# First convolution taps on ScalarE, more taps by adding transfers, and sevens in other groups of a hybrid attention and convolution block

## The chip, the cores and the metric

The kernel runs on one core of one Trainium2 chip. A core has TensorE (PE in the profile; PEld is its weight load), VectorE (DVE), ScalarE (ACT), GpSimd (POOL) and SyncE (SP). SP, ACT and POOL also issue transfers (DMA). The metric is the device time of one execution in microseconds; lower is better.

## The reference

One layer for 256 positions and width 4096, all in float32:

```python
xn = rms_norm(h, norm_in_g[i])
proj = xn @ w_in[i]                      # 4096 x 14336
q, k, v, z_a, a_c, g_c, z_c = split(proj)   # each 2048 wide
y_a = chunked_attention(q, k, v, rel_table[i])        # 16 heads of 128
y_a = rms_norm(y_a, attn_out_g[i]) * silu(z_a)
u = a_c * sigmoid(g_c)
u = causal_depthwise_conv(u, w_dw) + b_dw             # 31 taps
u = silu(layer_norm(u, ln_g, ln_b))
y_c = rms_norm(u @ w_pw + b_pw, conv_out_g[i]) * silu(z_c)
h = h + concatenate([y_a, y_c]) @ w_out[i]
gate = sigmoid(rms_norm(h, ple_norm_g[i]) @ w_ple_gate[i] + b_ple_gate[i])
h = h + gate * (p[i] @ w_ple[i])
return rms_norm(h, final_g)
```

## The kernel before

**Products.** A float32 operand is split into a high and a low part (`wh`, `wl` for weights, `big_t` for activations); a product of two blocks is three matmuls of 128x512 (high by high, low by high, high by low; line 428). ScalarE makes the high part by a cast, VectorE the low part by a subtraction (lines 204, 205). Weight parts have three buffers each.

**Groups.** `mixed_product` computes two column blocks of 512 over 16 pairs of k-blocks. A pair is done as an *eight* (8 block products, 24 matmuls) or, by Winograd's form of Strassen's method, as a *seven* (7 block products, 21 matmuls). A seven needs sums of weight blocks (`ua`, `ub`; VectorE, lines 526 to 540) and, for the activations, a combination (`xS`, `comb`), which has to be made beforehand. The string tables (`early`, `early_seven` and so on) give the order of the pairs in a group: a number with `*` is a seven whose sums VectorE makes, one with `+` a seven whose first sum comes from a plain transfer and an adding transfer on GpSimd's queue (line 471), a bare number an eight.

**Stages of the first half.** Ten groups follow one another: convolution chunk 0 (`glu_conv(0)`), chunk 1, query and key heads 0, value heads 0 and 1, chunk 2, query and key 1, chunk 3, query and key 2, query 3 with value 2, and key and value 3 (order `norm`). After the fourth, sixth, ninth and tenth group `attention(g)` runs for four heads: scores on TensorE, maxima on VectorE, exponential on ScalarE, transposes and values on TensorE, with copies on ScalarE between. After the tenth group and `attention(3)` comes the pointwise product (`w_pw`), whose left operand is `uS`, the split of the swish of the layer norm.

**The fill queue.** The convolution is 31 taps for each of 16 blocks of channels, on VectorE (`conv_tap`, lines 791 and 795). `glu_conv` puts a chunk's 124 taps into the queue `later`. After each pair of a group `fill(n)` takes the next `n` pieces from it; `n` comes from a table (`early_fills`, `six_fills`, `seven_fills`, `norm_fills`), one number for each pair. `layer_norm_swish` puts 71 pieces behind the taps: sums, the mean (a matmul), centering and squares, the variance (a matmul, and a power on GpSimd), its spread (a matmul), 16 swishes and 16 splits into `uS`, with empty places between. What is left after `attention(3)` is done by one `fill(len(later))`.

**Order.** A scheduler below the kernel interleaves the instructions of neighbouring pieces; each engine then runs its own in that fixed order and waits where it must. `behind_cast` places a piece behind the latest weight cast.

Of the kernel before, what the change touches and what calls it, by code (L numbers as in the profile page):

```python
# [10 lines left out]
F32 = mybir.dt.float32  # L11
F32R = mybir.dt.float32r
# [4 lines left out]
P = 128  # L17
# [8 lines left out]
def hybrid_block(  # L26
# [332 lines left out]
    early = units("1 3 5 0+ 7 9 2+ 11 13 4+ 15 8 6+ 10 12 14")  # L359
    early_five = units("1 3 5 0+ 7 9 2+ 11 4* 13 6+ 15 8* 10 12 14")  # L360
# [16 lines left out]

    def combine_into_places(pair, tiles):

        rows = sum_rows()  # L380
        places[pair] = spare_places(tiles[:4])
        t, i = tiles[pair // 2], pair % 2 * 2
        combine_again(None, None, t, i, rows, at_places=places[pair])()
# [266 lines left out]

    def first_pairs(add):
# [86 lines left out]
        later.extend(combinations(0))  # L738
        return n_x + 1, behind
# [49 lines left out]
    def conv_tap(cv, uT, i, b, k):  # L789
        if k == PAD:  # L790
            nc.vector.tensor_scalar(
                cv[:, i, :], uT[:, i, :], dw[:, b, k : k + 1], bdw[:, b : b + 1], ALU.mult, ALU.add
            )
        else:
            nc.vector.scalar_tensor_tensor(  # L795
                cv[:, i, PAD - k :], uT[:, i, : T + k - PAD], dw[:, b, k : k + 1],
                cv[:, i, PAD - k :], ALU.mult, ALU.add,
            )

    def comb_place(where, tag, **kw):  # L800
        return where.tile([P, 2, 2, T], F32R, tag=tag, name="comb_x", **kw), 0

    def more_combinations(pair):

        if pair in (7, 9, 11):
            c = (pair + 1) // 2
            xS[2 * c] = comb_place(act, "act") if c < 6 else comb_place(spool, "hd", bufs=5)
            later.extendleft(reversed(combinations(c)))

    def glu_conv(c):  # L810
# [4 lines left out]
        else:  # L815
            sg, gate = scaled_pair(
                w_in0, o_a + c * NB, o_g - o_a,
                *((early, r_x, early_fills) if c == 1 else (early_seven, r_x, seven_fills)),
                ahead=more_combinations if c == 2 else None,
# [616 lines left out]
```

## Time and profile before

| | |
|---|---|
| median of 3 runs | 2023.68 us (2023.65 to 2024.45) |
| the profiled execution's own time | 2023.59 us |
| its span in the trace | 2021.8 us |
| bytes by DMA | 450.86 MB, mean 223 GB/s |
| ACT_TABLE_LOAD instructions | 10, 1283 ns each |

A row of the groups reads: line, engine, operation, result <- operands, shapes, count | busy us, mean ns of one | idle time of the engine just before them and what ended it. A row of the windows reads: stretch, its length, busy us of PE, PEld, DVE, ACT, POOL with instruction counts, granted TensorE clock, DMA share, GB/s. A row of the timeline has start and length in us, engine, line and operation; neighbouring instructions of one kind are merged (xN), and an instruction's length holds a tail that overlaps the next one's start. A row of the waits reads: who waited <- for whom: us in total, times, longest.

### The profile page before, as it was taken

How to read it: one execution, taken by the hardware profiler on the slowest of the kernel's cores; microseconds unless marked ns; L12 is line 12 of the kernel's file. 1: busy time of each engine (PE TensorE's matmuls, PEld its weight loads, DVE VectorE, ACT ScalarE, POOL GpSimd, SP SyncE). 2: the span in 40 equal slices, each digit the busy share in tenths (PEclk: the TensorE clock that was granted, in tenths of full speed). 3: DMA queues.
4: the chain of work that ended last, by engine and by line, in shares of the span. 5: the costliest groups of instructions: out<-in, count | busy, mean ns of one | idle time of the engine just before them, and what ended most of it. 6: DMA issues, size and time to landing. Idle time of an engine off the chain costs nothing.

```text
span 2021.8 us, 26364 instructions
## 1 busy us (share of the span) xinstructions
PE 2003.7 (99%) x9043; PEld 1650.4 (82%) x9043; DVE 1920.5 (95%) x2759; ACT 1259.6 (62%) x1634; POOL 75.8 (4%) x83
## 2 busy tenths in 40 slices
PE   9999999999999999999999999999999999999997
PEld 7888888878888888788888888888888888888885
DVE  7999999899999999888999999999999999999997
ACT  7655555665666556776566676776666766566564
POOL 0000000000000000000000000000000000000000
PEclk9999999999999999999999999999999999999998
DMA  8788878678668877556686786876767766767675
GB/s 292 224 233 241 249 221 251 179 220 259 200 198 256 255 201 241 161 178 206 204 238 213 221 244 203 255 232 203 242 209 238 231 197 208 237 214 237 219 238 172
DMA packets 175920, 450.86 MB, mean 223 GB/s; under 512 B 14494, under 2 KB 17710, under 8 KB 175786
## 3 DMA queue, kind: packets, MB, share of 16 engines
q1 hardware_dynamic: 161952, 417.93, 63.6%
q0 software_dynamic: 13184, 30.41, 8.8%
q8 instruction: 71, 1.16, 0.2%
q10 hardware_dynamic: 650, 0.84, 0.1%
q14 instruction: 63, 0.52, 0.1%
HBM read 441.78 MB, written 4.19 MB: 221 GB/s over the span
## 4 chain that ended last, share of the span: by engine, by line
PE 93%; DVE 3%; DMA 2%; issue 2%; ACT 1%; POOLq 0%; POOL 0%; ACTq 0%; DVEq 0%
PE acc L428 70%; PE acc_P L428 18%; PE tmp_ps L170 1%; DVE wl L205 1%; PE acc L245 1%; DMA wt<-in_w_in_dram 1%; DVE cv L795 1%; DMA low<-in_w_in_dram 0%; DVE ul L205 0%; PE tmp_ps L967 0%; PE tmp_ps L951 0%; PE tmp_ps L985 0%; PE tmp_ps L990 0%; DMA wt<-in_w_ple_dram 0%; DMA wt<-in_w_ple_gate_dram 0%
## 5 line engine op out<-in xcount | busy, mean ns | idle before, releaser
L428 PE MATMUL acc<-wh,big_t 128*128 128x512 f32 x4028 | 1240.7, 391 | 0.9 <-DVE z L1146 0.9
L204 ACT CAST wh<-wt 128x1024 fp32r<-128x1024 f32 (+1 forms) x716 | 684.2, 965 | 460.9 <-PE acc L428 336.0
L428 PEld LDWEIGHTS acc<-wh,big_t 128*128 128x128 f32 x4028 | 753.5, 188 | 156.5 <-issue 1.0
L205 DVE TENSOR_TENSOR wl<-wt,wh 128x1024 fp32r<-128x1024 f32 (+1 forms) x716 | 787.9, 1112 | 30.0 <-ACT wh L204 24.8
L428 PE MATMUL acc<-wl,big_t 128*128 128x512 f32 x1958 | 760.3, 392 | 0.2 <-DVE wl L205 0.2
L428 PEld LDWEIGHTS acc<-wl,big_t 128*128 128x128 f32 x1958 | 367.4, 188 | 77.3 <-DVE wl L205 1.5
L204 ACT CAST uh<-ua 128x1024 fp32r<-128x1024 f32 x187 | 196.7, 1052 | 125.3 <-DVE ua L527 71.2
L205 DVE TENSOR_TENSOR ul<-ua,uh 128x1024 fp32r<-128x1024 f32 x187 | 228.0, 1219 | 6.7 <-ACT uh L204 5.1
L795 DVE SCALAR_TENSOR_TENSOR cv<-uT,dw,cv 128x255 f32<-128x255 f32 (+23 forms) x480 | 203.2, 461 | 1.1
L428 PE MATMUL acc_P<-uh,big_t 128*128 128x512 f32 x570 | 175.4, 389 | 0.0
L204 ACT CAST uh<-ub 128x1024 fp32r<-128x1024 f32 x99 | 104.2, 1053 | 51.6 <-DVE ub L540 36.8
L428 PEld LDWEIGHTS acc_P<-uh,big_t 128*128 128x128 f32 x570 | 107.0, 188 | 22.2
L205 DVE TENSOR_TENSOR ul<-ub,uh 128x1024 fp32r<-128x1024 f32 x99 | 120.7, 1219 | 0.5
L428 PE MATMUL acc_P<-ul,big_t 128*128 128x512 f32 x285 | 111.1, 390 | 0.0
L526 DVE TENSOR_TENSOR ua<-wt 128x512 f32<-128x512 f32 x112 | 76.7, 685 | 12.6 <-DMA wt<-in_w_in_dram 6.3
L428 PE MATMUL acc<-uh,big_t 128*128 128x512 f32 x286 | 88.5, 389 | 0.0
L428 PE MATMUL acc_P<-wh,big_t 128*128 128x512 f32 x286 | 88.2, 390 | 0.0
L527 DVE TENSOR_TENSOR ua<-wt 128x512 f32<-128x512 f32 x112 | 76.7, 685 | 4.7 <-DMA wt<-in_w_in_dram 3.5
L428 PE MATMUL acc_P<-uh,comb_t 128*128 128x512 f32 x228 | 70.2, 390 | 0.2 <-ACT uh L204 0.2
L540 DVE TENSOR_TENSOR ub<-ub,wt 128x512 f32<-128x512 f32 x99 | 68.1, 688 | 1.6
L539 DVE TENSOR_TENSOR ub<-ua,wt 128x512 f32<-128x512 f32 x99 | 67.7, 684 | 0.0
L428 PEld LDWEIGHTS acc_P<-ul,big_t 128*128 128x128 f32 x285 | 53.5, 188 | 12.1 <-DVE ul L205 1.0
(254 smaller groups left out, 1634.2 us busy)
## 6 DMA issues: line engine op xcount, KB each, us to landing
wt<-in_w_in_dram SPq DMA_DIRECT2D x416, 512.0 KB, 4.7
wt<-in_w_out_dram SPq DMA_DIRECT2D x128, 512.0 KB, 4.4
wt<-in_w_ple_gate_dram SPq DMA_DIRECT2D x128, 512.0 KB, 4.4
wt<-in_w_pw_dram SPq DMA_DIRECT2D x32, 512.0 KB, 4.5
ua<-in_w_in_dram SPq DMA_DIRECT2D x31, 512.0 KB, 4.3
ua<-in_w_in_dram POOLq DMA_DIRECT2D x31, 512.0 KB, 8.7
wt<-in_w_in_dram SPq DMA_DIRECT2D x31, 256.0 KB, 2.8
low<-in_w_in_dram POOLq DMA_DIRECT2D x12, 512.0 KB, 8.5
```

Source lines behind the costliest of these rows:

```text
L170: nc.tensor.transpose(pt[:, i * T + h * P : i * T + (h + 1) * P], src[:, h, b] if len(src.shape) == 4 else src[:, h, b * P : (b + 1) * P], ...
L204: nc.scalar.copy(wh[:, :kc, :], wt[:, :kc, :]),
L205: nc.vector.tensor_tensor(wl[:, :kc, :], wt[:, :kc, :], wh[:, :kc, :].bitcast(F32), ALU.subtract),
L245: nc.tensor.matmul(acc, a, b[:, k, :], start=kb == 0 and kind == 0, stop=kb == kblocks - 1 and kind == 2,)
L428: nc.tensor.matmul(banks[name], a, b, start=name not in begun, stop=final and ends[name] == n and kind == 2 and not (left and name in "P2 ...
L526: plus(ua[:, 0], w0[:, 0], w0[:, 1])
L527: plus(ua[:, 1], w0[:, 1], w1[:, 1])
L539: plus(ub[:, 0], ua[:, 0], w1[:, 1])
L540: plus(ub[:, 1], ub[:, 0], w1[:, 0])
L795: nc.vector.scalar_tensor_tensor(cv[:, i, PAD - k :], uT[:, i, : T + k - PAD], dw[:, b, k : k + 1], cv[:, i, PAD - k :], ALU.mult, ALU.add,)
```

## The change

- The first tap of each block (the one that also adds the bias) is done by ScalarE.
- In each chunk, blocks 2 and 3 get their taps 1 to 8 in another way: ScalarE multiplies into a tile (`tap`, two buffers shared with attention's `pT`), and a transfer on GpSimd's queue adds the tile to `cv`. One such piece stands behind every third tap of blocks 0 and 1; the remaining taps of blocks 2 and 3 come last, placed behind the latest VectorE tap.
- The combination of pair 8 is made in the first group, into spare places and a tile of its own; those of pairs 10 and 12 are made in chunks 2 and 3.
- Five groups (chunk 1, query and key 0, value 0 and 1, query and key 1, query and key 2) use `early_five` with five sevens in place of `early` with four; chunk 2 uses `early_six` in place of `early_seven`.
- The fill tables of these groups are new.

```diff
-    early_five = units("1 3 5 0+ 7 9 2+ 11 4* 13 6+ 15 8* 10 12 14")
+    early_five = units("1 3 5 0+ 7 9 2+ 11 8* 13 4+ 15 10 6* 12 14")
...
-    early_fills = (5, 6, 1, 5, 6, 1, 5, 6, 1, 5, 6, 1, 2, 5, 5, 4)
-    six_fills = (6, 6, 1, 5, 1, 5, 1, 5, 1, 5, 1, 5, 1, 6, 7, 7)
-    seven_fills = (6, 6, 1, 5, 1, 5, 1, 5, 1, 5, 1, 2, 5, 2, 5, 7)
+    five_fills = (5, 5, 1, 4, 5, 1, 4, 1, 5, 1, 4, 5, 1, 2, 5, 5)
+    third_fills = (5, 5, 4, 4, 4, 4, 5, 4, 4, 4, 4, 4, 4, 4, 5, 6)
+    early_fills = (5, 6, 1, 5, 6, 1, 5, 1, 5, 1, 4, 6, 1, 2, 6, 5)
+    six_fills = (6, 5, 1, 5, 1, 5, 1, 5, 1, 4, 1, 5, 1, 5, 6, 6)
+    seven_fills = (6, 5, 1, 5, 1, 5, 1, 5, 1, 5, 1, 2, 5, 2, 4, 7)
...
     def conv_tap(cv, uT, i, b, k):
         if k == PAD:
-            nc.vector.tensor_scalar(
-                cv[:, i, :], uT[:, i, :], dw[:, b, k : k + 1], bdw[:, b : b + 1], ALU.mult, ALU.add
+            nc.scalar.activation(
+                cv[:, i, :], uT[:, i, :], AF.Identity,
+                scale=dw[:, b, k : k + 1], bias=bdw[:, b : b + 1],
             )
...
+    def tap_by_dma(cv, uT, c, i, shift):
+
+        b = 4 * c + i
+        t = spool.tile([P, T], F32, tag="pT", name="tap")
+        nc.scalar.activation(
+            t[:, shift:], uT[:, i, : T - shift], AF.Identity,
+            scale=dw[:, b, PAD - shift : PAD - shift + 1],
+        )
+        nc.gpsimd.dma_start(cv[:, i, shift:], t[:, shift:], accum_op=ALU.add)
...
+    early_groups = {
+        1: (early_five, r_x, five_fills, None),
+        2: (early_six, r_x, third_fills, more_combinations(9, 10)),
+        3: (early_seven, r_x, seven_fills, more_combinations(11, 12)),
+    }
...
-        for i in range(4):
-            for k in reversed(range(TAPS)):
-                later.append(partial(conv_tap, cv, uT, i, 4 * c + i, k))
+        chain = {i: [partial(conv_tap, cv, uT, i, 4 * c + i, k) for k in reversed(range(TAPS))] for i in range(4)}
+        later.extend(chain[i].pop(0) for i in range(4))
+        rounds = deque((i, shift) for shift in range(1, BY_DMA + 1) for i in (2, 3))
+        for i in (2, 3):
+            del chain[i][:BY_DMA]
+        for n, work in enumerate(chain[0] + chain[1]):
+            later.append(work)
+            if n % 3 == 2 and rounds:
+                later.append(partial(behind_cast, tap_by_dma, cv, uT, c, *rounds.popleft()))
+        later.append(partial(behind_tap, chain[2].pop(0)))
+        later.extend(chain[2])
+        later.append(partial(behind_tap, chain[3].pop(0)))
+        later.extend(chain[3])
...
-    heads((o_q, 0), (o_k, 0))
-    heads((o_v, 0), (o_v, 1))
+    heads((o_q, 0), (o_k, 0), order=early_five, fills=five_fills)
+    heads((o_v, 0), (o_v, 1), order=early_five, fills=five_fills)
...
-    moved = comb_place(spool, "hd", bufs=5)
-    nc.scalar.copy(moved[0], xS[10][0])
-    xS[10] = moved
```

Counted over the program, TensorE has 12 matmuls of 128x512 less; VectorE 64 taps and 16 first taps less, 26 additions on 128x512 and 8 `ul` more; ScalarE 80 activations, 8 `uh` and 6 table loads more (16 in place of 10); GpSimd's queue 64 transfers more and 5 `ua` less.

The order of the instructions moves at the boundary between the tenth group and the pointwise product. On ScalarE, before, from the copies of the last key heads (`kT`) on, where `comb_u` is the combination of `uS` and `wh` a weight of the pointwise product:

```order
L956 COPY kT<-tmp_ps 128x512 x2
L298 CAST comb_u<-comb 128x2x256
L978 ACT_TABLE_LOAD
L978 ACTIVATE s,den<-s,nm 128x128
L978 ACTIVATE s,den<-s,nm 128x256
L204 CAST wh<-wt 128x1024
L987 COPY pT<-tmp_ps 128x384
L298 CAST comb_u<-comb 128x2x256
L204 CAST wh<-wt 128x1024
L994 ACTIVATE qT<-tmp_ps,den 128x128 x2
```

And now (line numbers of the changed kernel), where L966 is the swish, L1034 the exponential of attention, L1043 and L1050 its copies:

```order
L1012 COPY kT<-tmp_ps 128x512 x2
L966 ACT_TABLE_LOAD
L966 ACTIVATE cv<-cv,prm 128x256
L1034 ACT_TABLE_LOAD
L1034 ACTIVATE s,den<-s,nm 128x128
L1034 ACTIVATE s,den<-s,nm 128x256
L966 ACT_TABLE_LOAD
L966 ACTIVATE cv<-cv,prm 128x256
L1043 COPY pT<-tmp_ps 128x384
L966 ACTIVATE cv<-cv,prm 128x256 x3
L1050 ACTIVATE qT<-tmp_ps,den 128x128 x2
L966 ACTIVATE cv<-cv,prm 128x256 x2
```

The 16 swishes and the 16 splits stood ahead of the `kT` copies and now stand between the steps of the last four heads; the next weight cast comes behind all of them.

On TensorE at the same boundary, before (`acc_8124` to `acc_8127` belong to the pointwise product, L951 and L966 to L992 to attention):

```order
L951 MATMUL tmp_ps<-ident,z 128x128 x8
L428 MATMUL acc_8124<-wh,big_t 128x512 x2
L966 MATMUL tmp_ps<-kT,qT 128x128
L967 MATMUL tmp_ps<-kT,qT 128x256
L428 MATMUL acc_8124<-wl,big_t 128x512
L428 MATMUL acc_8126<-wh,big_t 128x512 x2
L428 MATMUL acc_8126<-wl,big_t 128x512
L428 MATMUL acc_8125<-wh,big_t 128x512 x2
L428 MATMUL acc_8125<-wl,big_t 128x512
```

And now (`acc_8296` is the pointwise product's first result; two more heads like the first stand where the line of the first values is followed by the last scores):

```order
L960 MATMUL tmp_ps<-lnsum,mean_w 128x128 x2
L1007 MATMUL tmp_ps<-ident,z 128x128 x8
L1022 MATMUL tmp_ps<-kT,qT 128x128
L1023 MATMUL tmp_ps<-kT,qT 128x256
L1041 MATMUL tmp_ps<-ident,s 128x128 x3
L1046 MATMUL tmp_ps<-z,pT 128x128
L1047 MATMUL tmp_ps<-z,pT 128x128
L1048 MATMUL tmp_ps<-z,pT 128x128
L1022 MATMUL tmp_ps<-kT,qT 128x128
L1023 MATMUL tmp_ps<-kT,qT 128x256
L1041 MATMUL tmp_ps<-ident,s 128x128 x3
```

The matmuls of the pointwise product stood between the steps of the heads and now stand behind the scores of the fourth head; the layer norm's spread (L960) stood in the middle of the tenth group and now at its end.

On GpSimd's queue, in the first conv chunks, before:

```order
L471 DMA ua<-in_w_in_dram 128x2x512 x6
L1017 MEMSET bias 64x4x64
L471 DMA ua<-in_w_in_dram 128x2x512 x11
L1017 MEMSET bias 64x4x64
L471 DMA ua<-in_w_in_dram 128x2x512 x7
```

And now:

```order
L476 DMA ua<-in_w_in_dram 128x2x512 x2
L837 DMA cv<-tap 128x255 x2
L837 DMA cv<-tap 128x254 x2
L476 DMA ua<-in_w_in_dram 128x2x512
L837 DMA cv<-tap 128x253 x2
L837 DMA cv<-tap 128x252 x2
L837 DMA cv<-tap 128x251
L476 DMA ua<-in_w_in_dram 128x2x512
L837 DMA cv<-tap 128x251
```

The adding transfers of the taps stand between those of the weight sums.

More of the change, by code (lines that the diff above doesn't have):

```diff
@@ L376, in hybrid_block, with combination_in_places @@
     places = {}
+    def combination_in_places(pair, tiles, rows, homes):
+        places[pair] = homes
+        t, i = tiles[pair // 2], pair % 2 * 2
+        return combine_again(None, None, t, i, rows, at_places=homes)
     def combine_into_places(pair, tiles):
[L380 to L383, printed above, removed]
+        combination_in_places(pair, tiles, sum_rows(), spare_places(tiles[:4]))()
     def mixed_product(
@@ L649, in combinations, with early_places, begin @@
         return begin, lambda: rest.pop()()
+    def early_places():
+        rest = []
+        def begin():
+            rows = spool.tile([P, 2, NB], F32, tag="stage", name="comb")
+            two = spool.tile([P, 2, 2, P], F32R, name="comb_p", bufs=1)
+            homes = spare_places(xT[:2]) + [[two[:, i, q] for q in range(2)] for i in range(2)]
+            rest.append(combination_in_places(8, xT, (rows[:, 0], rows[:, 1]), homes))
+        return begin, lambda: rest.pop()()
     def first_pairs(add):
@@ L1124, in hybrid_block @@
     r_c = rstd_of(ssq_c, CW, "r_c")
+    places.pop(8)
     xS = [xS[0][0]]
```

40 lines of the change are left out of this document (24 added, 16 removed).

## Prediction

> **What bounds the kernel now.** I read the page first: the busy shares, the groups, then the chain of work that ended last.
>
> ```profile
> span 2021.8 us, 26364 instructions
> PE 2003.7 (99%) x9043; PEld 1650.4 (82%) x9043; DVE 1920.5 (95%) x2759; ACT 1259.6 (62%) x1634; POOL 75.8 (4%) x83
> PE 93%; DVE 3%; DMA 2%; issue 2%; ACT 1%; POOLq 0%; POOL 0%; ACTq 0%; DVEq 0%
> L428 PE MATMUL acc<-wh,big_t 128*128 128x512 f32 x4028 | 1240.7, 391 | 0.9 <-DVE z L1146 0.9
> ```
>
> TensorE carries 93% of the chain that ended last, and its largest group waited 0.9 us in all. Next I asked for TensorE's own waits, the windows of single groups, and the chain in a stretch without a pause.
>
> ```profile
> PE acc_P L428 <- ACT uh L204: 1.6, 3, 0.9
> ...
> PE acc L428 <- DVE wl L205: 0.2, 1, 0.2
> 87.95 14.29 PE acc L428 x63
> 184.00:270.00 86.00, 86.00 (x385) 71.22 (x384) 86.00 (x142) 44.25 (x49) 5.17 (x5) 1.00 0.82 241
> 891.00:915.00 24.00, 23.95 (x130) 19.04 (x129) 17.14 (x39) 17.80 (x40) 0.00 (x0) 1.00 0.46 147
> ```
>
> The list of TensorE's waits has seven entries, 5.1 us together; no change to the other engines can win more than that. 63 matmuls follow one another in 14.29 us, so one costs 14.29 / 63 = 0.227 us. In a group of the projection (184 to 270) TensorE and VectorE are both busy for all 86 us. In 891 to 915, the boundary between the last projection group and the pointwise product, TensorE is busy for 23.95 of 24.00 us. That second window is the place that decides this forecast.
>
> **What the change removes from TensorE.** A seven takes 21 matmuls where an eight takes 24. Five groups go from four to five sevens (15 matmuls less), one conv group goes from seven to six (3 more): 12 less, 12 x 0.227 = **2.7 us**. This lies on the path and I count it in full.
>
> **VectorE, ScalarE and GpSimd in the projection groups.**
>
> ```profile
> L795 DVE SCALAR_TENSOR_TENSOR cv<-uT,dw,cv 128x255 f32<-128x255 f32 (+23 forms) x480 | 203.2, 461 | 1.1
> L791 DVE TENSOR_SCALAR cv<-uT,dw,prm 128x256 f32<-128x256 f32 x16 | 6.3, 407 | 0.9 <-ACT uT L835 0.9
> L526 DVE TENSOR_TENSOR ua<-wt 128x512 f32<-128x512 f32 x112 | 76.7, 685 | 12.6 <-DMA wt<-in_w_in_dram 6.3 <-DMA wt<-in_w_ple_gate_dram 4.5 <-DMA wt<-in_w_out_dram 1.6
> L205 DVE TENSOR_TENSOR ul<-ua,uh 128x1024 fp32r<-128x1024 f32 x187 | 228.0, 1219 | 6.7 <-ACT uh L204 5.1 <-PE acc L428 1.2
> ```
>
> VectorE loses 64 taps and 16 first taps (64 x 0.461 + 16 x 0.407 = 36 us) and gains 26 half-tile additions and 8 more `ul` (26 x 0.685 + 8 x 1.219 = 28 us; the other differences stay under 2 us): about 8 us less over nine groups. ScalarE gains 80 activations on 128x256 or less. The nearest row is the swish (596 ns, below), so 48 us, besides 8 `uh` and 6 table loads: some 60 us over 800 us in which it is busy for about half (44.25 of 86 us above), and TensorE waits for none of that as long as ScalarE stays up to three weight tiles ahead. The early combination of pair 8 adds two pieces to the first group, and the copy of `xS[10]` (ScalarE, about 1 us) goes; both lie in the same spare time. I cost all this at nothing. If the cover fails, or if VectorE's relief removes waits, it is worth at most the 5.1 us of waits downward, and upward what the third rival says.
>
> The 64 adding transfers are queued on GpSimd, behind and ahead of the transfers that form `ua`.
>
> ```profile
> hc<-z POOLq DMA_DIRECT2D x12, 256.0 KB, 6.1
> POOL ua L471 <- DMA ua<-in_w_in_dram: 320.5, 15, 50.4
> ```
>
> No row shows such a transfer of 128 KB. The nearest adds 256 KB from one tile to another and lands after 6.1 us; from below it is bounded by zero. A block's transfers follow one another every six entries of the fill queue. With 54 entries in 86 us that is 9.6 us, longer than 6.1, so I take them as hidden. `conv_tap` on VectorE waits for the last one, but 12 taps of blocks 0 and 1 stand between. Behind a late transfer would stand: on GpSimd the next `ua`, on ScalarE the tap two rounds later (two buffers), and behind that tap the weight casts.
>
> **What is moved: the layer norm.** This is the large term. The fill tables decide how many queued pieces are done in each group. Summed per table, the old ones drain 64, 64, 64, 58, 64, 58, 64, 63 in the eight groups ahead of the last one, the new ones 54, 54, 54, 70, 60, 56, 60, 58. The last group drains 71 in both. Before, 74 pieces are queued when it starts, so 3 are left; now 105, so 34 are left: 16 swishes, 16 splits, 2 empty places. `fill(len(later))` issues them behind the last head group of attention. The order shows what that does: the first matmul of the pointwise product needs the split of `uS`, so on TensorE it now stands behind three and a half heads of attention instead of between their steps. Before, the same place looks like this:
>
> ```profile
> 891.55 0.39 PE L428 MATMUL acc<-wl,big_t 128*128 128x512 f32 x1
> 891.78 1.03 PE L951 MATMUL tmp_ps<-ident,z 128*128 128x128 f32 x8
> 892.57 0.71 PE L428 MATMUL acc<-wh,big_t 128*128 128x512 f32 x2
> 892.70 1.07 ACT L956 COPY kT<-tmp_ps 128x512 f32<-128x512 f32 x2
> 893.33 0.49 PE L966 MATMUL tmp_ps<-kT,qT 128*128 128x128 f32 x2
> 893.66 0.60 PE L967 MATMUL tmp_ps<-kT,qT 128*128 128x256 f32 x2
> 893.90 0.58 PE L428 MATMUL acc<-wl,big_t 128*128 128x512 f32 x1
> 894.41 1.28 ACT L978 ACT_TABLE_LOAD   x1
> 895.71 0.40 ACT L978 ACTIVATE s<-s,nm 128x128 f32<-128x128 f32 x1
> 896.51 0.18 ACT L978 ACTIVATION_READ_ACCUMULATOR s<-s,nm 128x1 f32 x1
> 896.61 1.03 ACT L204 CAST wh<-wt 128x1024 fp32r<-128x1024 f32 x1
> 897.33 0.27 PE L985 MATMUL tmp_ps<-ident,s 128*128 128x128 f32 x1
> 897.91 0.38 PE L985 MATMUL tmp_ps<-ident,s 128*128 128x128 f32 x2
> 898.32 0.48 ACT L987 COPY pT<-tmp_ps 128x384 f32<-128x384 f32 x1 [0.68 <-PE tmp_ps L985]
> 898.70 0.62 ACT L298 CAST comb_u<-comb 128x512 fp32r<-128x512 f32 x1
> 899.27 0.38 PE L990 MATMUL tmp_ps<-z,pT 128*128 128x128 f32 x2
> 899.93 0.39 PE L966 MATMUL tmp_ps<-kT,qT 128*128 128x128 f32 x2
> 900.46 0.62 ACT L994 ACTIVATE qT<-tmp_ps,den 128x128 f32<-128x128 f32 x2
> 844.81 1.58 ACT L910 ACTIVATE cv<-cv,prm 128x256 f32<-128x256 f32 x3
> 875.65 2.25 ACT L920 CAST big_t<-cv 128x256 fp32r<-128x256 f32 x7 [0.41 <-PE acc L428]
> L618 ACT ACTIVATE junk<-qT 128x512 bf16<-128x512 f32 x8 | 5.1, 632 | 0.1
> ```
>
> Matmuls of the pointwise product (`acc` at 892.57, 893.90) fill each step of attention. In the changed order ScalarE goes through this chain between the `kT` copies and the third split, and no matmul of a product is left ahead of it on TensorE:
> - seven table loads, since swish and exponential alternate: 7 x 1.28 = 9.0
> - 16 swishes: three take 1.58 with the last one's tail, so one follows after (1.58 - 0.60) / 2 = 0.49: 7.8
> - three pairs of exponentials, 895.71 to 896.61: 3 x 0.90 = 2.7
> - three `pT` copies 3 x 0.48 = 1.4, three pairs of `qT` 3 x 0.62 = 1.9
> - three splits, seven take 2.25: 3 x 0.32 = 1.0
>
> Sum 23.8 us. It starts when the `kT` copies end, 893.77 - 891.94 = 1.8 us after the last matmul of the group, and gives the product's first matmul at 25.6 us. VectorE's part (16 multiplications and each head's maxima) fits beside it. TensorE's own work in that time is done before too: 8 transposes 1.0, four scores 4 x 0.57 (893.33 to 893.90), three heads' transposes 3 x 0.3 (one and two of them at 0.1) and values 3 x 0.66 (899.27 to 899.93), about 6.2 in all. So it stands idle for 25.6 - 6.2 = 19.4 us.
>
> Two tails follow. The three weight tiles that are ready give 36 matmuls (8.2 us) and the last head 1.0. ScalarE has more ahead of the next weight cast: 13 splits 4.2, a table load 1.3, the last head 0.9 + 0.5 + 0.6, two square sums 1.4 and two operand casts 1.1, then the cast's 1.05: 11.0 us. The difference is 1.8; some matmuls of the fourth tile start before the cast's tail is over, so I take 1.5. And the clock:
>
> ```profile
> 2008.00:2021.00 13.00, 0.79 (x7) 0.59 (x5) 5.11 (x13) 4.83 (x11) 0.93 (x1) 0.61 0.66 243
> 1.19 2.31 PE L125 MATMUL tmp_ps<-idle 128*128 128x512 bf16 x5 [1.19 <-DVE ssq_f L1241]
> ```
>
> After TensorE stops at about 2008 the granted clock of the window is 0.61, so it falls within the window; the first five matmuls of the program take 2.31 us, 0.46 each, about twice 0.227. If it falls in this pause too, some 6 us at half pace lose 3 us; if the heads' matmuls keep it up, nothing. I take the middle, 1.5. (The Trainium skill, "TensorE: Matmul & The Clock Gate", Part 1, states that the clock halves after an idle window of about 3.4 us and returns after as long a busy one. By that the loss would be 1.7 us. The rows agree with the fall; none here shows it in mid-kernel.)
>
> The Trainium skill speaks for a longer pause. Its "ScalarE: Activation LUTs", section "What ACT_TABLE_LOAD costs", adds a drain of 1.38 us to each load of 1.28 us. Here is the row against it:
>
> ```profile
> 841.43 1.05 ACT L204 CAST wh<-wt 128x1024 fp32r<-128x1024 f32 x1
> 842.50 1.28 ACT L910 ACT_TABLE_LOAD   x1
> ```
>
> The cast ends at 842.48, the load begins at 842.50, and there is no room for a drain. By the Trainium skill's figure the pause would be 7 x 1.38 = 9.7 us longer, and the time about 2052; I go by the row.
>
> **The sum.** 19.4 + 1.5 + 1.5 = 22.4, less about 0.6 us of small waits that the same stretch has now: 21.8 us. 2021.8 - 2.7 + 21.8 = 2040.9 us of span. The profiled run took 2023.59 for a span of 2021.8, 1.8 more, and lies 0.1 below the median of 2023.68. So **2042.5 us**, 0.9% slower.
>
> **The rivals.**
> - *A shorter pause* (chance 0.16). Some of the chain runs ahead: swishes before the last matmul, or loads that overlap a wait. Without two to seven of the loads, a few swishes and a tail it is 8 to 16 us on 2020.9: 2029 to 2037. For it: ScalarE has spare time (62%). Against it: `r_ln` needs a matmul that stands only 24 matmuls (5.4 us) ahead of the group's end, so no swish can begin much before that end.
> - *The cover holds* (0.06), the other side: the pieces left over cost TensorE nothing, and only the 2.7 us and at most the 5.1 us of waits remain: 2016 to 2021. It would need the chain to be shorter than the 6.2 us of attention beside it; it decides from there, and 23.8 is far from it. At -2.7 alone the change also would not do what it says it could: less VectorE work where TensorE already never waits buys nothing.
> - *Transfers that hold up ScalarE* (0.16). A `ua` that waits on GpSimd (up to 50.4 us now) keeps the taps behind it, the tap buffers stay full, and the casts stand behind a tap. TensorE has three weight tiles, 36 x 0.227 = 8.2 us; beyond 9.6 + 8.2 us it waits. At 2 to 5 us in each of four chunks this adds 8 to 20 us: 2050 to 2062. Against it: the order lets one to five taps pass between two `ua`.
>
> **How the numbers follow.** The forecast holds 0.62 (2037 to 2047). The range, 2031 to 2054, leaves out the cover's 0.06, a quarter of the shorter pause and some two thirds of the third rival, 0.2 together. A measurement tells about 0.2%, 4 us, from no change: below 2019.6 is faster, 0.02; within, 0.04; slower 0.94.
>
> **What would show it.** Right: a stretch of some 28 us near 890 to 920 in which TensorE is busy for less than a third, ScalarE without a pause in it, seven or eight table loads among swishes and exponentials; before that stretch TensorE as full as now. Wrong: matmuls of the pointwise product between the heads; or TensorE's idle time spread over the conv groups with GpSimd or a tap as the releaser; or a span below 2025, which would say that the chain overlaps the last group.

## The result, and the profile after

| | before | after |
|---|---|---|
| median of 5 runs each | 2023.68 us (2023.53 to 2024.45) | 2081.40 us (2078.66 to 2082.45) |
| ratio | | 1.0283, 95% interval 1.0268 to 1.0298 |
| profiled execution: time, span | 2023.59, 2021.8 us | 2082.29, 2080.5 us |
| end of the tenth group in the trace | 892.7 us | 929.5 us |
| from there to the end of the span | 1129.1 us | 1151.0 us |

The change makes the kernel 2.8% slower; the forecast was 0.9% slower. The "end of a group" here and below is the end of its last `z` row on VectorE (line 614, before: 609). The page of the changed kernel, with the rows that answer to those of before: shares, chain by engine, the largest group.

```profile
span 2080.5 us, 26533 instructions
PE 2022.9 (97%) x9031; PEld 1659.4 (80%) x9031; DVE 1922.3 (92%) x2716; ACT 1300.8 (63%) x1730; POOL 124.7 (6%) x142
PE 81%; DVE 7%; DMA 5%; issue 4%; ACT 3%; POOL 0%; POOLq 0%; ACTq 0%; DVEq 0%
L433 PE MATMUL acc<-wh,big_t 128*128 128x512 f32 x3972 | 1227.5, 393 | 3.0 <-ACT wh L204 1.8
```

The 12 matmuls are gone (9043 to 9031). But TensorE's share of the chain fell from 93% to 81%, and DVE, DMA, issue and ACT now hold 19% of it: time is lost in waits, not in work. The windows show where. The first is the stretch of the prediction's projection window, which now holds the end of the second group and most of the third; the second is the stretch behind the tenth group.

```profile
184.00:270.00 86.00, 82.30 (x350) 66.65 (x349) 76.74 (x111) 44.41 (x52) 7.08 (x8) 0.96 0.77 215
930.00:958.00 28.00, 13.99 (x47) 9.32 (x47) 12.30 (x38) 26.02 (x51) 0.00 (x0) 0.64 0.12 39
```

In the first, TensorE is busy for 82.30 us, where it was busy for all 86, and VectorE's busy time fell even more (76.74 for 86.00), by far more than its share of the 8 us of work that the change took from it over nine groups. Both engines now wait. In the second window ScalarE is busy for 26 of 28 us and TensorE for half, at a granted clock of 0.64: the pause that the prediction described. So there are two losses: **36.8 us in the first ten groups and 21.9 us behind them**, 58.7 us of span together.

**The second loss, as predicted.** A timeline of the changed kernel; the table loads of ScalarE between the last group and the first matmul of the pointwise product.

```profile
928.30 0.39 PE L433 MATMUL acc<-wl,big_t 128*128 128x512 f32 x1
930.81 1.28 ACT L966 ACT_TABLE_LOAD   x1
932.11 0.60 ACT L966 ACTIVATE cv<-cv,prm 128x256 f32<-128x256 f32 x1
932.73 1.28 ACT L1034 ACT_TABLE_LOAD   x1
935.02 1.28 ACT L966 ACT_TABLE_LOAD   x1
940.64 1.28 ACT L1034 ACT_TABLE_LOAD   x1
942.94 1.28 ACT L966 ACT_TABLE_LOAD   x1
949.04 1.28 ACT L1034 ACT_TABLE_LOAD   x1
951.34 1.28 ACT L966 ACT_TABLE_LOAD   x1
955.85 1.32 ACT L976 CAST big_t<-cv 128x256 fp32r<-128x256 f32 x4
956.92 2.40 PE L433 MATMUL acc<-wh,big_t 128*128 128x512 f32 x5 [0.34 <-ACT big_t L976]
```

Seven loads, switching between swish (line 966) and exponential (line 1034), then the splits, then the first product. Its five matmuls take 2.40 us, 0.48 each, about twice 0.227: the clock has fallen.

**The first loss, not predicted.** TensorE's waits in the ten groups, as in the waits of before: who <- for whom: us, times, longest.

```profile
PE tmp_ps L1007 <- DVE z L614: 16.1, 6, 8.4
PE acc_P L433 <- DVE ul L205: 3.3, 3, 1.9
PE acc L433 <- DVE wl L205: 2.7, 6, 0.6
PE tmp_ps L876 <- DVE z L869: 2.2, 2, 1.9
PE acc_P L433 <- ACT uh L204: 1.5, 2, 1.2
PE acc L433 <- ACT wh L204: 1.1, 2, 0.9
```

Together 26.9 us, against 2.0 in the same list of before (1.6, 0.2 and 0.2). The longest, 8.4 us, lies at the end of the sixth group. This is the timeline ahead of it, cut to the rows of the chain:

```profile
536.24 0.91 ACT L833 ACTIVATE tap<-uT,dw 128x252 f32<-128x252 f32 x2
540.36 1.22 POOL L476 DMA_DIRECT2D ua<-in_w_in_dram  x1 [9.99 <-DVE z L589]
541.09 1.44 POOL L837 DMA_DIRECT2D cv<-tap  x1
...
549.80 0.87 POOL L837 DMA_DIRECT2D cv<-tap  x1 [7.27 <-issue]
551.04 0.50 ACT L833 ACTIVATE tap<-uT,dw 128x251 f32<-128x251 f32 x1 [7.73 <-DMA cv<-tap]
...
552.67 2.92 ACT L204 CAST wh<-wt 128x1024 fp32r<-128x1024 f32 x3
553.73 1.23 DVE L205 TENSOR_TENSOR wl<-wt,wh 128x1024 fp32r<-128x1024 f32 x1 [7.68 <-ACT wh L204]
...
557.05 0.48 PE L1007 MATMUL tmp_ps<-ident,z 128*128 128x128 f32 x1 [8.40 <-DVE z L614]
```

Read from the bottom: TensorE waits for `z`, the result of the group that VectorE writes, and `z` stands on VectorE behind a `wl`; this waited 7.68 us for a weight cast; the casts stand on ScalarE behind a tap, which waited 7.73 us for a transfer, because both tap tiles were in use. The two products in these tiles began at 536.24. The first one's transfer was issued only at 541.09, behind a `ua` that GpSimd could issue no sooner than 540.36, and then took 9.9 us to land. A wait of 8 us at one tile went through three engines.

### The profile page after: what moved, and what is told of

It is laid out like the page before. It is cut to its first block, busy times and chain, and to the rows that moved or that the text cites. A ratio compares the mean times of both kernels' runs of the same rounds, so it can differ in the third digit from the quotient of the medians.

```text
span 2080.5 us, 26533 instructions
## 1 busy us (share of the span) xinstructions
PE 2022.9 (97%) x9031; PEld 1659.4 (80%) x9031; DVE 1922.3 (92%) x2716; ACT 1300.8 (63%) x1730; POOL 124.7 (6%) x142
## 4 chain that ended last, share of the span: by engine, by line
PE 81%; DVE 7%; DMA 5%; issue 4%; ACT 3%; POOL 0%; POOLq 0%; ACTq 0%; DVEq 0%
PE acc L433 61%; PE acc_P L433 16%; DVE wl L205 2%; DMA cv<-tap 2%; DMA wt<-in_w_in_dram 2%; DVE ul L205 1%; DVE cv L815 1%; PE tmp_ps L170 1%; DMA ua<-in_w_in_dram 1%; PE acc L245 1%; ACT wh L204 1%; DMA low<-in_w_out_dram 0%; PE tmp_ps L1007 0%; DVE z L614 0%; ACT L966 0%
## 5 line engine op out<-in xcount | busy, mean ns | idle before, releaser
L433 PE MATMUL acc<-wh,big_t 128*128 128x512 f32 x3972 | 1227.5, 393 | 3.0 <-ACT wh L204 1.8
L433 PEld LDWEIGHTS acc<-wh,big_t 128*128 128x128 f32 x3972 | 745.5, 189 | 160.9 <-ACT wh L204 3.6
L433 PE MATMUL acc<-wl,big_t 128*128 128x512 f32 x1930 | 749.9, 392 | 2.7 <-DVE wl L205 2.7
L204 ACT CAST uh<-ua 128x1024 fp32r<-128x1024 f32 x195 | 205.0, 1051 | 182.3 <-DVE ua L532 88.9
L205 DVE TENSOR_TENSOR ul<-ua,uh 128x1024 fp32r<-128x1024 f32 x195 | 237.7, 1219 | 8.2 <-ACT uh L204 7.8
L815 DVE SCALAR_TENSOR_TENSOR cv<-uT,dw,cv 128x243 f32<-128x243 f32 (+26 forms) x416 | 183.0, 462 | 7.3 <-DMA cv<-tap 3.4
L433 PE MATMUL acc_P<-uh,big_t 128*128 128x512 f32 x602 | 185.1, 389 | 0.0
L433 PE MATMUL acc_P<-ul,big_t 128*128 128x512 f32 x301 | 117.2, 390 | 0.2 <-DVE ul L205 0.2
L531 DVE TENSOR_TENSOR ua<-wt 128x512 f32<-128x512 f32 x121 | 82.9, 685 | 11.0 <-DMA wt<-in_w_in_dram 5.2
L532 DVE TENSOR_TENSOR ua<-wt 128x512 f32<-128x512 f32 x121 | 82.9, 685 | 7.1 <-DMA wt<-in_w_in_dram 6.5
L837 POOL DMA_DIRECT2D cv<-tap x64 | 58.0, 908 | 325.5 <-ACT tap L833 286.5
```

The source lines that it names most:

```text
L204: nc.scalar.copy(wh[:, :kc, :], wt[:, :kc, :]),
L205: nc.vector.tensor_tensor(wl[:, :kc, :], wt[:, :kc, :], wh[:, :kc, :].bitcast(F32), ALU.subtract),
L433: nc.tensor.matmul(banks[name], a, b, start=name not in begun, stop=final and ends[name] == n and kind == 2 and not (left and name in "P2 ...
L531: plus(ua[:, 0], w0[:, 0], w0[:, 1])
L532: plus(ua[:, 1], w0[:, 1], w1[:, 1])
L815: nc.vector.scalar_tensor_tensor(cv[:, i, PAD - k :], uT[:, i, : T + k - PAD], dw[:, b, k : k + 1], cv[:, i, PAD - k :], ALU.mult, ALU.add,)
```

## The experiments

All times are medians of their runs, and the ratios are to the kernel before on the same chip (2022.6 to 2025.7 us); "tenth group" and "after it" are the two parts of the span that the first table has, read from the one profiled execution of each run.

| run | us | ratio to before (95%) | tenth group ends | after it |
|---|---|---|---|---|
| before | 2023.7 | 1 | 892.7 | 1129.1 |
| after | 2081.4 | 1.0283 (1.0268 to 1.0298) | 929.5 | 1151.0 |
| r1 pieces run in the tenth group | 2071.1 | 1.0235 (1.0218 to 1.0252) | 940.1 | 1130.3 |
| r2 before, 34 pieces left over | 2045.5 | 1.0112 (1.0097 to 1.0127) | 891.3 | 1152.3 |
| r3 no adding transfers | 2047.9 | 1.0120 (1.0105 to 1.0136) | 894.7 | 1151.8 |
| r4 four tap tiles | 2057.5 | 1.0170 (1.0155 to 1.0186) | 903.9 | 1151.6 |
| r5 no transfers, pieces spread | 2031.5 | 1.0030 (1.0019 to 1.0042) | 902.0 | 1128.5 |
| r6 four tiles, pieces spread | 2036.7 | 1.0056 (1.0041 to 1.0071) | 907.8 | 1129.8 |
| r7 more descriptor space | 2081.6 | 1.0275 (1.0257 to 1.0294) | 928.6 | 1151.4 |
| r8 half the transfers | 2072.2 | 1.0230 (1.0214 to 1.0245) | 919.8 | 1151.1 |
| r9 products on GpSimd | 2097.8 | 1.0367 (1.0349 to 1.0385) | 942.6 | 1151.7 |
| r10 four sevens, transfers | 2070.8 | 1.0225 (1.0207 to 1.0242) | 917.0 | 1155.5 |
| r11 four sevens, no transfers, spread | 2029.3 | 1.0025 (1.0015 to 1.0035) | 897.1 | 1128.1 |
| r12 taps put off behind ua | 2090.1 | 1.0332 (1.0317 to 1.0347) | 934.0 | 1153.4 |
| r13 the same, four tiles | 2059.6 | 1.0178 (1.0161 to 1.0195) | 905.4 | 1153.0 |
| r14 the same, four tiles, spread | 2033.5 | 1.0051 (1.0036 to 1.0066) | 902.2 | 1128.3 |
| r15 no adding half of ua | 2062.1 | 1.0188 (1.0173 to 1.0203) | 908.7 | 1151.0 |
| r16 half the transfers, twice as far apart | 2054.6 | 1.0155 (1.0139 to 1.0172) | 898.9 | 1153.3 |

The theories: A, the pieces left over make the boundary pause. C, the adding transfers hold up ScalarE: C1, because there are only two tap tiles; C2, because GpSimd can't issue the next transfer. D, a starred seven whose combination is new makes VectorE late. The rival to A was that the pause comes from what the ten groups do.

### The boundary: r1 and r2

```diff
# r1, the changed kernel: the tenth group runs 31 pieces more
-    norm_fills = (7, 8, 8, 8, 6, 4, 2, 3, 2, 3, 2, 2, 0, 6, 5, 5)
+    norm_fills = (9, 10, 10, 10, 8, 6, 4, 5, 4, 5, 4, 5, 3, 8, 7, 7)
# r2, the kernel before: the tenth group runs 31 pieces less
-    norm_fills = (7, 8, 8, 8, 6, 4, 2, 3, 2, 3, 2, 2, 0, 6, 5, 5)
+    norm_fills = (3, 0, 0, 0, 3, 4, 2, 3, 2, 3, 2, 2, 0, 6, 5, 5)
```

> The changed kernel, with only the fill table of the tenth group enlarged (105 pieces in place of 71), so that no swish and no split is left for the boundary. Theory A (the pause of 21.9 us behind the tenth group comes from the 34 pieces left over): the span from the tenth group's end to the end of the program falls from 1151.0 us to 1129 to 1132, and the time to 2058 to 2063. Rival B (that part is longer for another reason, such as late weights or the clock): it stays above 1145 and the time above 2075. The part up to the tenth group stays within 3 us, or grows by up to 5 because VectorE then has 92 us of work in that group.

> The kernel before, with only the fill table of its tenth group cut to 40 pieces, so that 34 are left for the boundary as in the changed kernel; no tap is moved. Theory A: the pause appears here too, 2043 to 2048 us (20 to 24 us more than before). Rival B: it needs the taps by transfer or the other sevens, and the time stays below 2030.

r2 moves no tap and no seven, and has the pause: the stretch behind the tenth group grows from 1129.1 to 1152.3 us. Its window there is the changed kernel's over again:

```profile
891.30:919.30 28.00, 14.29 (x50) 9.37 (x49) 12.31 (x37) 26.02 (x53) 0.00 (x0) 0.57 0.12 39
```

r1 has no pause (1130.3), so A holds from both sides and its rival falls. But r1 was some 8 us slower than expected: its tenth group takes 103.8 us in place of 93.4, with a wait of TensorE that the changed kernel doesn't have:

```profile
928.05 1.65 PE L433 MATMUL acc<-wh,big_t 128*128 128x512 f32 x3 [5.93 <-ACT wh L204]
```

The pieces cost ten of the 21 us again when one group has to take them all.

### Whether the transfers make the first loss: r3, r4, r7

```diff
# r3: all taps but the first on VectorE
-    BY_DMA = 8
+    BY_DMA = 0
# r4: the second block's taps use the two tiles of attention's s
-        t = spool.tile([P, T], F32, tag="pT", name="tap")
+        t = spool.tile([P, T], F32, tag=("pT", "s")[i % 2], name="tap")
# r7: descriptor space
-dynamic_dma_scratch_size=1024
+dynamic_dma_scratch_size=1536
```

> The changed kernel with no taps by transfer (BY_DMA = 0): those 64 taps are VectorE's again, the first taps stay on ScalarE, the sevens and the fill tables stay. Theory C (the tap transfers hold up ScalarE, which waits for a free tap tile with the weight casts behind it): the 36.8 us that the first ten groups are late fall to 5 to 15, though VectorE gets 24 us more work, and the time is 2050 to 2062. Rival D (VectorE is late at the sevens whose sums it makes itself): the first ten groups stay as late or get later, 2080 or more.

> The changed kernel with two tap tiles for each of the two blocks (four in place of two; the second pair is shared with attention's score tiles). Theory C1 (the number of tap tiles is what ScalarE waits for): ScalarE's waits for tap transfers fall from 31.1 us to under 10 and the time to 2058 to 2068. Theory C2 (GpSimd cannot issue the next transfer until an earlier one has landed, whatever the tiles): the waits fall less, and the time is 2068 to 2080. Rival D: no change, 2079 to 2083.

> The changed kernel with descriptor space for GpSimd's transfers of 1536 instead of 1024; the order of all instructions is the same. If GpSimd's idle time of 5.9 to 7.3 us before a tap's issue is a wait for descriptor space (C2) and sets the delays: that idle time goes, 2060 to 2074. If the two tap tiles set the delays (C1), or GpSimd waits for something else than this space: 2078 to 2084, with four or five such idle times as before.

Without transfers the tenth group ends at 894.7 us: **34.8 of the 36.8 us go with them** and with ScalarE's products for them, more than was expected (2.0 us stay, where 5 to 15 were to stay). All the sevens of the change are still in, so D by itself is not a large cause. The groups of VectorE's weight splits in the ten groups tell how late the casts come: idle time before them, and how much of it a cast ended. Before:

```profile
L205 DVE TENSOR_TENSOR wl<-wt,wh 128x1024 fp32r<-128x1024 f32 (+1 forms) x288 | 324.4, 1136 | 7.6 <-ACT wh L204 4.8 <-ACT qT L994 2.3
```

After:

```profile
L205 DVE TENSOR_TENSOR wl<-wt,wh 128x1024 fp32r<-128x1024 f32 (+1 forms) x289 | 322.9, 1129 | 44.8 <-ACT wh L204 44.1
```

r3:

```profile
L205 DVE TENSOR_TENSOR wl<-wt,wh 128x1024 fp32r<-128x1024 f32 (+1 forms) x289 | 323.5, 1131 | 3.6 <-ACT wh L204 3.2
```

r4, with VectorE's taps:

```profile
L205 DVE TENSOR_TENSOR wl<-wt,wh 128x1024 fp32r<-128x1024 f32 (+1 forms) x289 | 323.2, 1131 | 19.7 <-ACT wh L204 19.3
L815 DVE SCALAR_TENSOR_TENSOR cv<-uT,dw,cv 128x243 f32<-128x243 f32 (+26 forms) x416 | 183.5, 464 | 9.1 <-DMA cv<-tap 5.3 <-ACT cv L809 0.3
```

The work is the same in all of them; the idle time goes from 4.8 to 44.1, and without transfers to 3.2. Four tiles take back 25.6 us, and ScalarE's wait for a free tile falls. In the waits of the changed kernel, then of r4:

```profile
ACT tap L833 <- DMA cv<-tap: 31.1, 13, 7.7
```

```profile
ACT tap L833 <- DMA cv<-tap: 2.7, 1, 2.7
```

The transfers themselves land no sooner with four tiles: least, median and most are 2.6, 4.9 and 9.9 us after, 2.6, 5.0 and 10.5 in r4. It is the wait for a tile that costs, and not the landing as such.

r7 tells apart what GpSimd's 7.27 us of "issue" were. At the same place, first GpSimd, then ScalarE:

```profile
540.29 1.22 POOL L476 DMA_DIRECT2D ua<-in_w_in_dram  x1 [9.98 <-DMA ua<-in_w_in_dram]
541.03 2.31 POOL L837 DMA_DIRECT2D cv<-tap  x2
551.25 0.87 POOL L837 DMA_DIRECT2D cv<-tap  x1 [7.91 <-ACT tap L833]
```

```profile
550.39 0.50 ACT L833 ACTIVATE tap<-uT,dw 128x251 f32<-128x251 f32 x1 [7.66 <-DMA cv<-tap]
```

With more space GpSimd issues both taps at once behind `ua`, and the pause for "issue" is gone; yet ScalarE's tap still waits 7.66 us and the time stays. So the space did hold GpSimd up, but the time did not depend on it, and C2 falls as far as the descriptor space goes. What r7 leaves in place is GpSimd's wait for a `ua`: the products whose transfer stands behind one wait for their issue, four of them for 4.1 to 4.7 us in the trace of the changed kernel, five for 3.7 to 5.9 us in r7's.

### What makes a tile come back late: r8, r16, r12, r13, r15

```diff
# r8: four shifts rather than eight
-    BY_DMA = 8
+    BY_DMA = 4
# r16: r8, and a tap behind every sixth piece
-            if n % 3 == 2 and rounds:
+            if n % 6 == 5 and rounds:
# r12, r13 (with r4's tiles), r14: in sums_ahead and in fill
+                hold[0] = 2
...
+            if hold[0] and getattr(work, "func", None) is behind_cast:
+                put_off.append(work)
# r15
-                nc.gpsimd.dma_start(ua, columns(col, step + apart), accum_op=ALU.add)
```

> The changed kernel with four adding transfers a block instead of eight: 32 in all, the other 32 taps back on VectorE. Per transfer the same price (34.8 us / 64 = 0.54 us): 2081.4 - 17.4 = 2064, so 2059 to 2069. If only the pile-up of the later rounds with the ua transfers costs: under 2055. If a few transfers delay as much as all (one late tap per group is enough): over 2072.

> Half the transfers (32) as in r8, but one for every six pieces rather than every three, so that the tiles have twice the time. If the transfers' spacing sets the loss: r8's 2072.2 falls to 2050 to 2060. If single transfers that land late are enough, however far apart (behind a ua at the end of a group): 2066 to 2076.

Half the transfers save only 9.7 of the 34.8 us (the time lies 0.2 us inside the third answer): the price is not so much for each. The same half at twice the distance saves 30.6. In r8 ScalarE waited 9.5 us for tiles (the longest 6.2), and in two places VectorE's own tap stood waiting for the last sum, which TensorE then felt. In this one the transfer was issued at 351.5, behind a `ua`, and took 10.1 us to land:

```profile
361.62 0.99 DVE L815 SCALAR_TENSOR_TENSOR cv<-uT,dw,cv 128x251 f32<-128x251 f32 x2 [5.91 <-DMA cv<-tap]
...
365.97 0.77 PE L433 MATMUL acc<-wh,big_t 128*128 128x512 f32 x1 [6.30 <-DVE z L614]
```

A few late transfers do it, and room between them heals most of it.

> The changed kernel, but a tap that would go to the queue in the same or the next unit after a ua transfer was issued is put off until that is over (other pieces of the queue run in its place). Two tap tiles as before. If the long waits come from taps that stand behind a ua in GpSimd's DMA queue (three of the four longest ScalarE waits, 6.5, 7.7 and 4.1 us, follow one): they go, the tenth group ends at 900 to 915 and the time is 2052 to 2067. If two tiles are too few wherever the taps stand: 2072 to 2085, since the taps put off come closer together.

> The same with four tap tiles. Four tiles alone gave 2057.5, no transfers at all 2047.9. If what is left of the transfers with four tiles (9.6 us) is taps behind ua: 2046 to 2051. If it is work that the taps put on ScalarE and the waits of VectorE's own taps for the last sum: 2055 to 2060.

> The changed kernel without the adding half of the ua transfers (a plus-marked seven then works with one column block in place of the sum of two; that part of the computation is left out). All 64 taps' transfers, the two tiles and the matmuls stay; only nothing else adds in GpSimd's queue in these groups. If a tap behind a ua is what lands late and holds the two tiles: ScalarE's wait for a tile falls from 31 us to under 10, the tenth group ends at 895 to 908, the time is 2047 to 2062. If the two tiles are too few in any case: 2070 to 2083.

r12 failed to do what it was for, and its time lies above both answers. GpSimd stood idle for 9.77 us ahead of this `ua`, whose tile has to be free and hold its first half, so a tap put off by two units stood right behind it again. The taps put off also came closer together: ScalarE's waits for a tile grew from 31.1 to 50.3 us.

```profile
541.57 1.22 POOL L487 DMA_DIRECT2D ua<-in_w_in_dram  x1 [9.77 <-DVE wl L216]
542.30 1.44 POOL L849 DMA_DIRECT2D cv<-tap  x1
```

r13 falls into its second answer (2059.6, beside r4's 2057.5), but since the taps still stood behind `ua` it can't tell what a tap away from `ua` is worth. r15 takes the neighbour away: all 64 taps, two tiles, but no other adding transfer in these groups, since it leaves out the second half of each such `ua`. The first row is ScalarE's wait for a tile, the second the landing of the taps (least, median, most):

```profile
ACT tap L832 <- DMA cv<-tap: 12.1, 10, 3.5
```

```profile
DMA to landing us min/median/max: 2.6/4.4/7.2
```

No tap lands after more than 7.2 us, TensorE's waits of 8.4 and 6.1 us are gone, and 20.8 us come back; the wait for a tile and the time (2062.1) came out just above what was expected. It is not that `ua` itself is ready sooner: ScalarE waits for no `ua` transfer in either kernel. In the trace of the changed kernel the same two kinds of taps can be told apart: 11 of the 64 were issued while a `ua` was on its way, and landed 4.8 to 9.9 us later (median 7.0), the other 53 after 2.6 to 7.0 (median 4.2). And in r15 no product waits more than 1 us for its issue. So the long waits need both: a tap that stands behind a `ua`, for its issue and then on its way, and only two tiles. How much of it is the issue and how much the way, no run separates. Either remedy takes most of the loss away. With one of them 9 to 14 us are left; r4's waits put some of it on casts that come late all the same (19.3 us) and on VectorE's taps that wait for the last sum (5.3 us). That part was not settled.

### Where the product is made, and the fifth seven: r9, r10

```diff
# r9
-        nc.scalar.activation(
-            t[:, shift:], uT[:, i, : T - shift], AF.Identity,
-            scale=dw[:, b, PAD - shift : PAD - shift + 1],
-        )
+        nc.gpsimd.tensor_scalar(
+            t[:, shift:], uT[:, i, : T - shift], dw[:, b, PAD - shift : PAD - shift + 1], None, ALU.mult
+        )
# r10: early in place of early_five, in all five groups
-    heads((o_q, 1), (o_k, 1), order=early_five)
+    heads((o_q, 1), (o_k, 1))
...
```

> The changed kernel with the product of each tap on GpSimd instead of ScalarE; tiles (two), transfers and the places in the queue stay. So a product that waits for a free tap tile holds up GpSimd's queue, no longer ScalarE's, where the weight casts stand behind it. If ScalarE's queue is what turns a late landing into lost time: the weight casts' wait goes back to some 25 us and the time to 2046 to 2060, whatever GpSimd takes for a product. If the late landings themselves cost (VectorE's further taps, which wait for the last sum): 2072 to 2085. If GpSimd's product is so slow (over 3 us for one) that the taps come later still: over 2085.

> The changed kernel with its transfers, but five of the groups with four sevens as before (five in the changed kernel), so 12 matmuls more for each seven that goes and less VectorE work; pieces left over stay 34. If the transfers cost by themselves: 2078 to 2088 (35 us less nothing, plus the matmuls that come back). If they cost only because the fifth seven has taken VectorE's slack, so that a late cast can't be made up: 2045 to 2060.

r9 is inconclusive. Its time lies in the answer for products of over 3 us, but GpSimd takes 0.89 to 6.76 us with a median of 1.49 (ScalarE takes 0.50), and since `ua` is queued behind these products, ScalarE now waits for `ua`:

```profile
ACT uh L204 <- DMA ua<-in_w_in_dram: 27.0, 3, 12.9
```

The hold-up only moved to another queue. r10 came between its two answers: with four sevens in five groups (three matmuls more for each, not twelve: 15, or 3.4 us) the ten groups end 12.5 us sooner. That fits a slack of VectorE that makes up part of the late casts and that the fifth seven takes, but doesn't prove it: ScalarE waits for tiles as long in all (30.8 us), while the longest wait fell from 7.7 to 4.7. 24.3 us over before stay.

### All losses treated: r5, r6, r11, r14

The 31 pieces are spread over the eight groups ahead of the tenth, one entry at a time:

```diff
-    five_fills = (5, 5, 1, 4, 5, 1, 4, 1, 5, 1, 4, 5, 1, 2, 5, 5)
+    five_fills = (5, 5, 2, 4, 5, 2, 4, 2, 5, 2, 4, 5, 1, 2, 5, 5)
-    early_fills = (5, 6, 1, 5, 6, 1, 5, 1, 5, 1, 4, 6, 1, 2, 6, 5)
+    early_fills = (5, 6, 2, 5, 6, 2, 5, 2, 5, 2, 4, 6, 1, 2, 6, 5)
...
```

> The changed kernel without adding transfers (all taps but the first on VectorE) and with 31 more pieces of the queue run before the boundary, spread over the eight groups ahead of the tenth (four more each, three in the third chunk's group) rather than all in the tenth. If the two losses are the transfers (34.8 us) and the 31 pieces left over (21.9 us) and nothing else: 2081.4 - 34.8 - 21.9 = 2024.7; I expect 2023 to 2030, with 1129 to 1132 us behind the tenth group and its end at 892 to 898. Rival (the pieces cost as much in any group as they did in the tenth, 10.6 us for 31): 2034 to 2038.

> The changed kernel with four tap tiles and the same 31 pieces spread over eight earlier groups. If the boundary pause goes and nothing is given back: 2057.5 - 21.9 = 2035.6, so 2034 to 2040. Rival (more pieces at each matmul group make the taps fall closer together, and the tiles and transfers are late more often): 2040 to 2055, with the tenth group's end later than the 903.9 that four tiles alone gave.

> The kernel of r5 (no transfers, the 31 pieces spread) with four sevens in those groups. r5 came out 6.8 us over its 2024.7, with VectorE busy 94.5 of 96 us in its sixth group and 85.6 of 87 in its third. If the work of the fifth seven on VectorE does that: 2022 to 2027, with the tenth group's end at 890 to 896. If the 31 spread pieces do it: 2029 to 2034 as in r5.

> Four tap tiles, taps kept off ua, and the 31 pieces spread over eight earlier groups: all three losses treated at once, with all 12 matmuls saved. If they are all: 2021 to 2027, no more than 2.7 us under before. If the fifth sevens and the spread pieces bind VectorE and ScalarE to each other as in r6: 2031 to 2038.

r6 met its expectation: the pause goes (1129.8), and 3.9 us are given back at the tenth group (907.8, beside r4's 903.9). r5 did not: 2031.5 in place of 2023 to 2030, and below its rival's 2034. Its tenth group ends 7.3 us later than r3's. Its fourth and seventh group (the expectation of r11 counts them without the first), and the same two of before:

```profile
272.40:359.30 86.90, 86.90 (x387) 71.80 (x387) 85.54 (x137) 48.64 (x56) 3.65 (x3) 1.00 0.74 221
537.70:633.60 95.90, 93.69 (x430) 74.98 (x428) 94.40 (x157) 61.47 (x92) 2.44 (x2) 1.00 0.65 189
```

```profile
271.60:358.10 86.50, 86.50 (x387) 71.71 (x386) 86.18 (x146) 45.50 (x52) 4.87 (x4) 1.00 0.80 231
534.90:628.20 93.30, 92.84 (x430) 75.88 (x430) 90.47 (x141) 59.65 (x88) 2.44 (x2) 1.00 0.66 200
```

In the longer of the two VectorE is busy for 94.40 of 95.9 us, and TensorE waits for 2.2 us of it. r11 tests whether the fifth sevens' work on VectorE does that: it takes them out. In the profiled execution, one of the fastest, its tenth group ends 4.9 us sooner; but its median, 2029.3 (2026.8 to 2032.3 in nine runs), missed 2022 to 2027 and lies in the answer for the spread pieces, and its ratio to before can't be told from r5's. So the fifth seven explains a part at best; the rest of the 6 us stays open.

r14, at 1.0051, lies in its second answer. It was to treat all losses at once, but as r12 shows, putting the taps off does not take them away from `ua`, and it can't be told from r6 (1.0056). **No version beat the kernel before**, and the 12 matmuls that go, 2.7 us, are 0.13% of the time.

## Why the prediction was wrong

By its own steps:

- **TensorE's 2.7 us**: right in kind, the 12 matmuls went. But r3, without transfers, is 2.0 us later at the tenth group than before: TensorE's waits in its ten groups are 5.2 us, against 2.0 before, so even there waits had eaten the gain.
- **The layer norm that is moved**: right, in mechanism and size. 21.8 us forecast; 21.9 measured, and 23.2 in r2, where nothing else was changed. Seven table loads, 16 swishes, no product before 956.9. That the sum hit to 0.1 us is partly luck all the same. The first product was to come 23.8 us after the `kT` copies; after 930.79 (the copies' end) it came at 956.92, 26.1: ScalarE waited 0.26, 0.75 and 0.75 us for the heads' values, which the chain had left out. Both tails were too large: the wait for the next weight cast was 0.72 us (1.5 forecast), and the granted clock from 956.92 to 960.30 was 0.78, which loses some 0.7 us, worked out (1.5 forecast). About 1 us of the difference has no row. (The last step from span to time also has a slip: 2040.9 and 1.8 and 0.1 make 2042.8, not 2042.5; nothing hangs on it.)
- **Drains of table loads**: the activation at 932.11 ends at 932.71 and the load begins at 932.73, so the row was the right choice. By the Trainium skill ("ScalarE: Activation LUTs", "What ACT_TABLE_LOAD costs") the pause would have been 9.7 us longer; it was not.
- **The 64 transfers, "hidden"**: this is the step that failed. The prediction set a mean distance of 9.6 us between two transfers of a block against a median landing of 6.1 us. The distance was even counted too short: from one transfer of a block to the next are eight entries of the queue, six taps and two transfers, so 12.7 us; in the trace the median is 12.5. And the median landing was shorter, 4.9 us. But a tile is waited for in the worst case and not in the middle one: a transfer behind a `ua` took up to 9.9 us to land after up to 4.7 us of waiting for its issue, and 8 of the 56 distances are under 6.1 us, the least 3.7 (r8 beside r16 shows what distance does). The step also took what ScalarE gains "at nothing" because it is half idle, where a wait in its queue counts and not its work.
- **The third rival** named that path (a `ua` that waits on GpSimd, taps behind it, full tiles, casts behind a tap), with a chance of 0.16, and priced it at 8 to 20 us. It cost 34.8. Three things were missing in the price. How often: 13 waits for a tile, not one in each of four chunks. The cover: it let TensorE wait only beyond 9.6 + 8.2 us, 8.2 of them for three weight tiles that are ready; but at the end of a group TensorE waits for `z`, which stands on VectorE behind a `wl`, so ready weights don't help. 16.1 of the 26.9 us are waits for `z` at the end of a group, and in the case shown 7.7 us at the tile became 8.4 on TensorE. And the engines can't catch up: in the ten groups VectorE waited 44.1 us for casts, and with four sevens (r10) 12.5 us came back, though 15 matmuls (3.4 us) were added.
- **The clock**: forecast for the pause, with 1.5 us. It also fell in mid-kernel, which no term had. These are five stretches of the changed kernel, in or right behind waits of TensorE; the number after the five engines is the granted clock.

```profile
149.45:152.85 3.40, 3.40 (x10) 2.61 (x9) 3.40 (x7) 0.30 (x1) 0.06 (x1) 0.50 0.94 237
193.83:197.20 3.37, 3.37 (x12) 2.88 (x13) 2.10 (x2) 2.04 (x4) 0.87 (x1) 0.50 0.89 203
241.61:245.00 3.39, 3.39 (x10) 2.62 (x9) 3.39 (x6) 0.00 (x0) 0.00 (x0) 0.50 0.74 226
552.30:562.40 10.10, 5.17 (x20) 4.59 (x21) 8.03 (x11) 6.23 (x9) 0.45 (x1) 0.50 0.36 91
743.40:750.20 6.80, 5.28 (x20) 4.70 (x21) 6.80 (x12) 3.24 (x5) 0.86 (x1) 0.50 0.60 137
```

TensorE is busy for 20.6 us in them at half the pace: some 10.3 us lost, worked out. With the 24.9 us of waits more than before that makes 35.2 of the 39.5 us (36.8 and the 2.7 saved) that the ten groups lost; 4.3 us have no row. In the ten groups of before and of r3 the granted clock is 1.00.

## What to carry to other kernels

A step put on an engine that others wait for is priced by the longest wait it can bring into that engine's queue, not by its work or by a median landing: look for the transfer that will stand in front of it, and count the buffers against that one. Work that is moved out of a stretch has to be placed where an engine is free, in small portions; at a boundary it cost 22 us, in one group 10, spread over eight 4 (r6) to 7 (r5). And ask first what there is to win: here 0.13%.

## What was not expected of the hardware

- An adding transfer of some 126 KB that was issued while a `ua` was on its way in the same queue landed after 4.8 to 9.9 us (median 7.0, 11 of 64), the others after 2.6 to 7.0 (median 4.2); without `ua` (r15) none took more than 7.2.
- GpSimd's pause for "issue" ahead of such a transfer (7.27 us at 549.80) went with more descriptor space, though the time didn't change (r7).
- The clock fell to 0.50 for 3.4 us behind waits of TensorE of 1.20, 1.85 and 1.85 us (at 148.5, 193.1 and 241.3). The Trainium skill ("TensorE: Matmul & The Clock Gate", Part 1) names an idle window of about 3.4 us as what halves it; the length of the low stretch agrees with that figure, the length of the wait before it does not. A wait of 1.24 us at 636.6 left the clock at 1.00, so the length alone doesn't decide it.
